# Token-block sums put off, and second-stage loads tied to product numbers, in a one-core encoder layer

## The chip, the cores and the metric

The kernel runs on one core of one Trainium2 chip. The metric is the device time of the whole program in microseconds, from runs on the chip. The profile is one execution taken by the hardware profiler, with its times counted from the first instruction of the span.

## What is computed

One layer of an encoder on x of 512 tokens and 1024 columns, in float32:

```
x = x + 0.5 * ffn1(rms(x));  x = x + mixer(rms(x));  x = x + 0.5 * ffn2(rms(x));  x = rms(x)
ffn(h) = (silu(h @ w_gate) * (h @ w_up)) @ w_down        # 1024 -> 2816 -> 1024
```

The mixer is chunked attention beside a pooling mixer, with one input and one output projection. The change does not touch it. It touches the two down projections, `@ w_down`, and the first norm.

## The kernel before

**Numbers.** A float32 operand is split into a high part that TensorE takes as it is and a low rest: ScalarE casts the high part (`split`, L157), VectorE subtracts it (L158). A product of two operands is three matmuls: high by high, high by low, low by high (`mm3`, L274, L275, L276).

**The down projection.** Its inputs are four token blocks A11, A12, A21, A22 (two halves of the tokens by two halves of the 2816 inner columns) and four weight blocks. The class `Down` forms the result from seven block products with sums of blocks (a scheme of the Strassen kind). Sums of weight blocks, T1 to T4, are made in DRAM by DMAs from POOL's queue (`make_sums`, L939; tile `wsum`). Sums of token blocks, S1 to S4, are made by VectorE. Each block product runs over six groups of the inner dimension (`G` is 6). A group holds two blocks of 128 inner rows, the last holds one, so its products are half as long. Products are counted by `n_products`:

- 1 to 18: for each group g the products S2 by T2, A11 by B11, S1 by T1, into the accumulators `p6`, `p1`, `p5`
- 19 to 30: S3 by T3 (into `p7`) and S4 by B22 (into `p5`), in turn, so 19, 20, 22, 24, 26, 28 are S3
- 31 to 36: A12 by B21 (into `p1`)
- 37 on: A22 by T4 (into `p7`), then the last residual sums, the final norm and the output

**One product.** `product` calls `operands`: `weights` fetches a weight block with a DMA on SP's queue (L965, L968; tile `raw`, up to ten buffers in turn) and splits it into `whi`, `wlo`; `tokens` splits a token block into a pair `ah`, `ah`. Then come the matmuls (`mms`). `tokens` did one thing more: right after the split of S2 and of A11 of a group it issued a sum on VectorE that the later products need, S2 - A12 into S2 (this is S4) or S3 + A11 into S3:

```
if i in (S2, A11):
    dst, other, op = (S2, A12, ALU.subtract) if i == S2 else (S3, A11, ALU.add)
    ...
    nc.vector.tensor_tensor(dst, dst, other, op=op)        # L1002
```

That is two sums for each of six groups, twelve in each stage.

**Buffers.** Token pairs take two buffers of the pool `norm` (tag `h`, 16 buffers of one size). In the second stage the eight rows `xt` of the residual, reloaded from DRAM (`x_d`), take one buffer each of the same pool and keep it. Split weights have four places (`part_tiles`).

**Order.** A tile framework schedules instructions by a model of their times, and inserts the waits. Inside `tc.manual_schedule(engines=...)` the named engines keep the program's order. In products 1 to 18 of both stages, and in the rest of the first stage, SP keeps it; in products 19 on of the second stage SP was scheduled freely. VectorE, ScalarE and TensorE are scheduled freely in the products, but not in the up stage ahead of them. `tc.issue_after(ins)` ties the instructions in its block behind `ins` on the engine of `ins`.

**Reloads.** `self.loads` is a list of DMAs that `product` issues on SP behind the product's weight load (L1028): in the second stage one at each product past 4 whose number leaves 0 or 2 when divided by 3, so 5, 6, 8, 9, 11, 12, 14, 15 for `xt[6]`, `xt[7]`, `xt[2]`, `xt[4]`, `xt[3]`, `xt[5]`, `xt[0]`, `xt[1]`, and 17, 18 for the two rows of the final gain (`gb`). In the first stage it is the input x, one tile each at 15, 18, up to 36. Behind product 19 VectorE scales and adds the accumulators (`scaled`, L1037; `residual`, L1769, into `xt[6]` and `xt[7]`). One piece of `todo` behind each of products 20 to 25 then adds `u2` into `xt[2]`, `xt[4]`, `xt[6]`, `xt[3]`, `xt[5]`, `xt[7]`.

**First norm.** In the opening, `read_in` makes 24 times three matmuls over three pairs of input blocks and lists the last matmul of each three in `made`. The sums of the norm over rows (`per_token`, L389, eight matmuls of one column) are tied behind `made[14]`, the broadcast over rows (`spread`, L414, two matmuls on the scaled identity of L405) behind `made[19]`.

Of the kernel before, what the change touches and what calls it, by code (L numbers as in the profile page):

```python
# [9 lines left out]
F32 = mybir.dt.float32  # L10
# [3 lines left out]
ALU = mybir.AluOpType  # L14
# [3 lines left out]
P = 128  # L18
D = 1024
S = 512  # L20
# [38 lines left out]
STEP, SWITCH, TURN = 0.02, 0.32, 0.11  # L59
ACT_FIX, DVE_FIX, QK_NORM, NORM = 0.09, 0.1, 3.7538, 3.08  # L60
AHEAD_AT = 8
FIRST_NORM = 14, 19
OPENING = (
    "B0 W1 n0 n1 n2 W2 p W3 p B1 p6 W4 W5 B2 p B3 g0 p2 g1 u0 u1 W6 P20 O1 p m0 p W7 P21 g2 m1 p u2 "
    "L0 m2 L1 F0 F1 h0 F2 h1 F3 p2 h2 p L2 h3 p h4 L3 g3 h5 p O0 F4 "
# [11 lines left out]
def layer(  # L77
# [71 lines left out]
            what(*args)  # L149


    last_cast = [None]

    def split(src, hi, lo, scale=None):

        if scale is None:
            last_cast[0] = nc.scalar.copy(hi, src)  # L157
            nc.vector.tensor_tensor(lo, src, hi.bitcast(F32), op=ALU.subtract)  # L158
        else:
            last_cast[0] = nc.scalar.activation(hi, src, AF.Copy, scale=scale)  # L160
            nc.vector.scalar_tensor_tensor(
                lo, src, scale, hi.bitcast(F32), op0=ALU.mult, op1=ALU.subtract
            )

# [717 lines left out]
    class Down:  # L882
# [36 lines left out]

        def begin(self, pool):  # L920
            self.pool, self.acts = pool, []
            self.raws, self.parts, self.pairs = {}, {}, {}
            self.n_products, self.loads, self.loads_from, self.load_turns = 0, [], 4, (0, 2)
            self.open(range(1))
            rooms[:] = [
                z for tag in ("ra", "rb") for z in ((wpool, "raw", RAW, 1024), (pool, tag, RAW, 2 * S))
            ]
            part_rooms[:] = [(wpool, HILO)] * HILO + [(pool, 1)]
# [59 lines left out]
        def tokens(self, i, g, scale=None):  # L988

            if (i, g) in self.pairs:  # L990
                return self.pairs.pop((i, g))
            n = groups[g][1]
            src = self.acts[g][:, S2 if i == S4 else i].rearrange("p k c -> p (k c)")
            pair = [hpool.tile([P, 2, HT], F32R, tag="h", name=name("ah")) for _ in range(2)]
            split(src, *(z[:, :n, :].rearrange("p k c -> p (k c)") for z in pair), scale)
            if i in (S2, A11):

                dst, other, op = (S2, A12, ALU.subtract) if i == S2 else (S3, A11, ALU.add)
                dst, other = (
                    self.acts[g][:, j].rearrange("p k c -> p (k c)") for j in (dst, other)  # L1000
                )
                nc.vector.tensor_tensor(dst, dst, other, op=op)  # L1002
            return pair

        def mms(self, acc, g, a, w, tts=(0, 1), further=False):
# [9 lines left out]

        def operands(self, g, a, i, scale=None):
            w = self.weights(i, g)
            return self.tokens(a, g, scale), w

        def product(self, acc, g, a, i, further=False, scale=None):  # L1020
            a, w = self.operands(g, a, i, scale)
            self.n_products += 1
            if self.n_products == 12:
                tables(AF.Abs_reciprocal_sqrt, a[0][:, 0, 0:1].bitcast(F32))
            turn = self.n_products % 3
            if self.n_products > self.loads_from and turn in self.load_turns and self.loads:
                dst, src = self.loads.pop(0)
                nc.sync.dma_start(dst, src)  # L1028
            if turn == 1 and self.n_products > 1 and self.steps:
                self.make_sums(last_cast[0], 1)  # L1030
            self.mms(acc, g, a, w, further=further)

    def whole(make):
        return [[(make(), 0, S)] for _ in range(2)]
# [37 lines left out]
    with tc.tile_pool(name="act1", bufs=1, reuse_waits="tile") as apool:  # L1072
        down1.begin(apool)
        down1.open(range(1, G - 3))
        ffn_up(n1, wA1, down1, False)
        p1, p5, p6 = whole(bank), whole(bank), whole(abank)

        with tc.manual_schedule(engines={mybir.EngineType.SP}):
            for g in range(G):
                down1.product(p6, g, S2, T2)  # L1080
                down1.product(p1, g, A11, B11)
                down1.product(p5, g, S1, T1)
                if g == 0:

                    x[:] = residual_tiles()
                    half = KD // 2
                    down1.loads = [(x[k], xT[k]) for k in (*range(half, KD), *range(half))]
                    down1.loads_from, down1.load_turns = 14, (0,)
        with tc.manual_schedule(engines={mybir.EngineType.SP}):
            p7 = whole(abank)  # L1090
            u2 = halved(p6)

            y = [down1.acts[i // 2][:, i % 2].rearrange("p k c -> p (k c)") for i in range(2 * NT)]
            down1.product(p7, 0, S3, T3)
            for tt in range(2):
                scaled(u2[tt], p1[tt][0][0], 0.5, u2[tt], ALU.subtract)
                scaled(y[NT + 2 + tt], p5[tt][0][0], 0.5, u2[tt])
            for g in range(G):
                if g + 1 < G:
                    down1.product(p7, g + 1, S3, T3)  # L1100
                down1.product(p5, g, S4, B22, further=True)

            def add(d):

                tp = bank() if d >= KD // 2 else abank()
                for t in range(NT):
                    nc.tensor.transpose(
                        tp[:, t * P : (t + 1) * P],
                        y[d // 4 * NT + t][:, d % 4 * P : (d % 4 + 1) * P], ident,
                    )  # L1110
                nc.vector.tensor_tensor(x[d], x[d], tp, op=ALU.add)
                n2.add(d)

            for tt in range(2):
                todo.append((scaled, y[NT + tt], p5[tt][0][0], -0.5, u2[tt], ALU.subtract))
                todo.append((scaled, y[NT + 2 + tt], p7[tt][0][0], 0.5, y[NT + 2 + tt]))
            for g in range(G):
                down1.product(p1, g, A12, B21, further=True)
                piece()
            todo.extend((add, d) for d in range(KD // 2, KD))  # L1120
            for tt in range(2):
                nc.scalar.activation(two(y[tt]), back(p1[tt][0][0]), AF.Copy, scale=0.5)
            ahead = down1.operands(0, A22, T4, -1.0)
            for g in range(G):
                a, w = ahead
                if g + 1 < G:
                    ahead = down1.operands(g + 1, A22, T4, -1.0)
                down1.mms(p7, g, a, w, further=True)
                piece()
            for tt in range(2):  # L1130
                scaled(y[2 + tt], p7[tt][0][0], -0.5, u2[tt], ALU.subtract)
            for d in range(KD // 2):
                add(d)
        rooms[:] = [(wpool, "raw", RAW, 1024)]
# [595 lines left out]
    with tc.tile_pool(name="act2", bufs=1, reuse_waits="tile") as apool:  # L1730
# [107 lines left out]
        with tc.manual_schedule(engines={mybir.EngineType.SP}):  # L1838
            for g in range(G):
                down2.product(p6, g, S2, T2)  # L1840
                down2.product(p1, g, A11, B11)
                down2.product(p5, g, S1, T1)
                if g == 0:
                    down2.loads = [(xt[i], x_d[i]) for i in (6, 7, 2, 4, 3, 5, 0, 1)] + [
                        (z, final_gain[:, i * S : (i + 1) * S].to_broadcast([P, S]))
                        for i, z in enumerate(gb)
                    ]

        p7 = whole(abank)
        u2 = halved(p6)  # L1850
        down2.product(p7, 0, S3, T3)
        for tt in range(2):
            scaled(u2[tt], p1[tt][0][0], 0.5, u2[tt], ALU.subtract)
            residual(1, 2 + tt, p5[tt][0][0])
            for i in (2 + tt, NT + tt, NT + 2 + tt):
                op = ALU.subtract if i < NT + 2 else ALU.add
                todo.append((nc.vector.tensor_tensor, xt[i], xt[i], u2[tt], op))
        for g in range(G):
            if g + 1 < G:
                down2.product(p7, g + 1, S3, T3)  # L1860
                piece()
            down2.product(p5, g, S4, B22, further=True)
            piece()
        piece(len(todo))
        for tt in range(2):
            todo.append((residual, 1, tt, p5[tt][0][0], 0, S, -0.5))
            todo.extend((residual, 1, 2 + tt, *at) for at in p7[tt])
            todo.append((settle, 1, tt, 1))
            todo.append((settle, 1, 2 + tt, 1))
        for g in range(G):  # L1870
            down2.product(p1, g, A12, B21, further=True)
            piece(2)
        piece(len(todo))
        for tt in range(2):
            residual(0, tt, p1[tt][0][0])
            settle(0, tt, 0)
# [141 lines left out]
```

## Time and profile before

| what | value |
|---|---|
| median of 3 runs | 808.35 us (807.63 to 808.61) |
| the profiled execution | 808.83 us, its span 807.0 us |
| busy: TensorE matmul, weight load, VectorE, ScalarE, POOL | 797.8, 735.5, 710.3, 503.8, 100.1 us |
| granted TensorE clock, mean | 0.999 of full speed |
| first down stage, product 1 to the end of its matmuls | about 219 to 324 us |
| second down stage, product 1 to the end of its matmuls | about 700 to 800 us |

Busy times are sums over instructions, and matmuls overlap in them: a matmul of 512 columns is shown with 0.38 us, though the next one starts 0.22 us later. So a short wait of TensorE shows as a longer step between two starts rather than as idle time. The time outside the span, 808.83 - 807.0, is the program's start and end.

### The profile page before, as it was taken

What the parts mean: (1) busy time and instruction counts of PE and PEld (TensorE: products, weight loads), DVE (VectorE), ACT (ScalarE), POOL (GpSimd) and SP (SyncE); (2) the same over time, 40 slices, a digit from 0 to 9 for tenths busy, and PEclk for the clock granted to TensorE, in tenths of its full rate; (3) what the DMA queues carried; (4) which work ended last, traced back from release to release, by engine and by line L of the source; (5) the groups of instructions that cost most, each with busy time, mean ns of one, the idle gap of its engine ahead of it and who ended that gap; (6) DMA issues with size and microseconds to landing.
All of it is one profiled execution on the core that took longest, in us unless ns stands there. A gap on an engine that the chain in (4) does not pass through costs nothing.

```text
span 807.0 us, 14153 instructions
## 1 busy us (share of the span) xinstructions
PE 797.8 (99%) x5273; PEld 735.5 (91%) x5273; DVE 710.3 (88%) x1163; ACT 503.8 (62%) x873; POOL 100.1 (12%) x148
## 2 busy tenths in 40 slices
PE   9999999999999999999999999999999999999996
PEld 8889999999988888888878888899999999988886
DVE  7999999899897878876979778999989999896997
ACT  8456555666676657558657756565566655766574
POOL 0111111222011100101111000201121111010100
PEclk9999999999999999999999999999999999999999
DMA  8677778988799973332212137858878888799942
GB/s 311 184 210 203 185 214 247 208 201 216 200 270 314 310 241 105 118 118 92 78 54 79 53 132 250 268 160 224 216 213 230 213 199 210 222 305 339 320 144 104
DMA packets 79414, 160.61 MB, mean 199 GB/s; under 512 B 7393, under 2 KB 30705, under 8 KB 78961
## 3 DMA queue, kind: packets, MB, share of 16 engines
q1 hardware_dynamic: 56256, 113.16, 41.7%
q0 software_dynamic: 22656, 46.14, 27.2%
q8 instruction: 41, 0.67, 0.3%
q10 hardware_dynamic: 432, 0.41, 0.1%
q14 instruction: 29, 0.23, 0.1%
HBM read 153.38 MB, written 50.34 MB: 252 GB/s over the span
## 4 chain that ended last, share of the span: by engine, by line
PE 86%; DVE 7%; ACT 4%; issue 2%; DMA 1%; SPq 0%; DVEq 0%; ACTq 0%
PE mm L274 20%; PE mm L275 20%; PE mm L276 20%; PE a L276 7%; PE a L275 7%; PE a L274 7%; DVE wlo L158 1%; PE a L1518 1%; PE a L1506 1%; ACT prob L1423 1%; ACT prob L1429 1%; ACT whi L1235 1%; PE a L1454 1%; DVE prob L1416 1%; DVE wlo L1237 1%
## 5 line engine op out<-in xcount | busy, mean ns | idle before, releaser
L158 DVE TENSOR_TENSOR wlo<-raw,whi 128x1024 fp32r<-128x1024 f32 (+1 forms) x110 | 120.6, 1107 | 17.7 <-ACT whi L157 17.6
L157 ACT CAST whi<-raw 128x1024 fp32r<-128x1024 f32 (+1 forms) x110 | 103.2, 951 | 38.1 <-PE mm L276 14.8
L939 POOL DMA_DIRECT2D wsum<-in_wB_dram x72 | 70.2, 1086 | 447.8 <-DVE t L843 222.1
L275 PE MATMUL mm<-ha,whi 128*128 128x256 f32 x420 | 115.5, 275 | 0.0
L276 PE MATMUL mm<-ha,wlo 128*128 128x256 f32 x420 | 115.5, 275 | 0.0
L274 PE MATMUL mm<-ha,whi 128*128 128x256 f32 x420 | 115.5, 275 | 0.0
L788 ACT ACTIVATE t<-mm 128x256 f32<-128x256 f32 x105 | 40.4, 385 | 113.6 <-PE mm L276 113.1
L600 DVE TENSOR_TENSOR wlo<-wsum,whi 128x1024 fp32r<-128x1024 f32 x70 | 85.5, 1221 | 9.8 <-ACT whi L595 9.8
L274 PEld LDWEIGHTS mm<-ha,whi 128*128 128x128 f32 x420 | 80.6, 192 | 0.1
L275 PEld LDWEIGHTS mm<-ha,whi 128*128 128x128 f32 x420 | 80.6, 192 | 0.1
L276 PEld LDWEIGHTS mm<-ha,wlo 128*128 128x128 f32 x420 | 80.6, 192 | 0.0
L595 ACT CAST whi<-wsum 128x1024 fp32r<-128x1024 f32 x70 | 70.0, 1047 | 3.7 <-DVE wsum L619 2.0
L275 PE MATMUL mm<-wlo,ah 128*128 128x512 f32 x176 | 67.0, 380 | 0.1
L276 PE MATMUL mm<-whi,ah 128*128 128x512 f32 x176 | 66.7, 379 | 0.0
L274 PE MATMUL mm<-whi,ah 128*128 128x512 f32 x176 | 66.5, 379 | 0.0
L274 PE MATMUL mm<-hhi,whi 128*128 128x512 f32 x168 | 64.5, 384 | 0.0
L600 DVE TENSOR_TENSOR wlo<-raw,whi 128x512 fp32r<-128x512 f32 x70 | 64.1, 955 | 0.0
L275 PE MATMUL mm<-hlo,whi 128*128 128x512 f32 x168 | 63.7, 379 | 0.0
L276 PE MATMUL mm<-hhi,wlo 128*128 128x512 f32 x168 | 63.7, 379 | 0.0
L595 ACT CAST whi<-raw 128x512 fp32r<-128x512 f32 x70 | 57.9, 828 | 1.9 <-PE mm L275 1.9
L158 DVE TENSOR_TENSOR ah<-acts,ah 128x512 fp32r<-128x512 f32 (+1 forms) x72 | 45.7, 646 | 10.9 <-ACT ah L157 10.8
L157 ACT CAST ah<-acts 128x512 fp32r<-128x512 f32 (+1 forms) x72 | 40.6, 581 | 20.4 <-PE mm L275 13.8
(246 smaller groups left out, 2331.6 us busy)
## 6 DMA issues: line engine op xcount, KB each, us to landing
raw<-in_wA_dram SPq DMA_DIRECT2D x142, 256.0 KB, 3.9
wsum<-in_wB_dram POOLq DMA_DIRECT2D x60, 512.0 KB, 7.2
raw<-wsum SPq DMA_DIRECT2D x40, 512.0 KB, 6.3
raw<-in_wB_dram SPq DMA_DIRECT2D x30, 512.0 KB, 8.4
wsum<-wsum POOLq DMA_DIRECT2D x20, 512.0 KB, 5.7
raw<-in_wA_dram SPq DMA_DIRECT2D x16, 512.0 KB, 4.6
x<-in_xT_dram SPq DMA_DIRECT2D x16, 256.0 KB, 6.4
raw<-in_wQK_dram SPq DMA_DIRECT2D x8, 512.0 KB, 3.4
```

What stands on the lines that cost most here:

```text
L157: last_cast[0] = nc.scalar.copy(hi, src)
L158: nc.vector.tensor_tensor(lo, src, hi.bitcast(F32), op=ALU.subtract)
L274: nc.tensor.matmul(acc, a[0], b[0], start=start, stop=False, **more)
L275: nc.tensor.matmul(acc, a[0], b[1], start=False, stop=False, **more)
L276: return nc.tensor.matmul(acc, a[1], b[0], start=False, stop=stop, **more)
L595: nc.scalar.copy(hi, src)
L600: nc.vector.tensor_tensor(lo, src, hi.bitcast(F32), op=ALU.subtract)
L788: nc.scalar.activation(two(dst), back(src), AF.Copy, scale=scale)
L939: begun = nc.gpsimd.dma_start(self.rows(i, g), self.rows(self.terms[i][at], g), **(dict(accum_op=ALU.add) if at else {}),)
L1235: nc.scalar.copy(hi, raws[i])
L1237: nc.vector.tensor_tensor(lo, raws[i], hi.bitcast(F32), op=ALU.subtract)
L1416: nc.vector.tensor_tensor_reduce(p, sc, bias[h][0][:, S - n :], -1.0, BIG, op0=ALU.add, op1=ALU.min, accum_out=nm)
```

## The change

It has four parts. The token-block sums are no longer issued in `tokens`; they are put into a list `put_off`, and from the seventh product on each call of `operands` takes one from it and ties it behind the last low-part subtraction (`last_low`). The reloads are given by a table from product number to DMA: in the second stage `RELOADS`, in the first stage 15 + 3 i. Products 19 to 36 of the second stage now stand inside the manual order of SP. The first entry of `FIRST_NORM` goes from 14 to 15.

```diff
-FIRST_NORM = 14, 19
+FIRST_NORM = 15, 19
+RELOADS = 5, 6, 16, 17, 22, 23, 26, 27, 29, 30
...
     def split(src, hi, lo, scale=None):
...
-            nc.vector.tensor_tensor(lo, src, hi.bitcast(F32), op=ALU.subtract)
+            last_low[0] = nc.vector.tensor_tensor(lo, src, hi.bitcast(F32), op=ALU.subtract)
...
-            nc.vector.scalar_tensor_tensor(
+            last_low[0] = nc.vector.scalar_tensor_tensor(
...
         def begin(self, pool):
...
-            self.raws, self.parts, self.pairs = {}, {}, {}
-            self.n_products, self.loads, self.loads_from, self.load_turns = 0, [], 4, (0, 2)
+            self.raws, self.parts, self.pairs, self.put_off = {}, {}, {}, []
+            self.n_products, self.loads = 0, {}
...
         def tokens(self, i, g, scale=None):
...
-                nc.vector.tensor_tensor(dst, dst, other, op=op)
+                self.put_off.append((dst, dst, other, op))
...
         def operands(self, g, a, i, scale=None):
             w = self.weights(i, g)
-            return self.tokens(a, g, scale), w
+            a = self.tokens(a, g, scale)
+            if self.n_products > 5 and self.put_off:
+                *z, op = self.put_off.pop(0)
+                with tc.issue_after(last_low[0].ins):
+                    nc.vector.tensor_tensor(*z, op=op)
+            return a, w
...
         def product(self, acc, g, a, i, further=False, scale=None):
...
-            if self.n_products > self.loads_from and turn in self.load_turns and self.loads:
-                dst, src = self.loads.pop(0)
-                nc.sync.dma_start(dst, src)
+            if self.n_products in self.loads:
+                nc.sync.dma_start(*self.loads[self.n_products])
...
-                    down1.loads = [(x[k], xT[k]) for k in (*range(half, KD), *range(half))]
-                    down1.loads_from, down1.load_turns = 14, (0,)
+                    down1.loads = {
+                        15 + 3 * i: (x[k], xT[k]) for i, k in enumerate((*range(half, KD), *range(half)))
+                    }
...
         with tc.manual_schedule(engines={mybir.EngineType.SP}):
...
                 if g == 0:
-                    down2.loads = [(xt[i], x_d[i]) for i in (6, 7, 2, 4, 3, 5, 0, 1)] + [
-                        (z, final_gain[:, i * S : (i + 1) * S].to_broadcast([P, S]))
-                        for i, z in enumerate(gb)
-                    ]
+                    down2.loads = {
+                        n: (xt[i], x_d[i]) for n, i in zip(RELOADS, (6, 7, 2, 4, 3, 5, 0, 1))
+                    } | {
+                        n: (z, final_gain[:, i * S : (i + 1) * S].to_broadcast([P, S]))
+                        for i, (n, z) in enumerate(zip(RELOADS[8:], gb))
+                    }
...
```

What follows in the second stage, from `p7 = whole(abank)` to the `piece(len(todo))` behind products 31 to 36, is moved inside that `with` block line by line, and is otherwise the same.

## Rows read from the trace of the kernel before

**Rows 1.** The page's busy time by engine, and a costly group (busy, mean ns).

```profile
PE 797.8 (99%) x5273; PEld 735.5 (91%) x5273; DVE 710.3 (88%) x1163; ACT 503.8 (62%) x873; POOL 100.1 (12%) x148
...
L157 ACT CAST whi<-raw 128x1024 fp32r<-128x1024 f32 (+1 forms) x110 | 103.2, 951 | 38.1 <-PE mm L276 14.8
```

**Rows 2.** Timeline of TensorE, second down stage (start us, duration us).

```profile
712.99 0.59 PE L274 MATMUL mm<-whi,ah 128*128 128x512 f32 x2
713.71 0.48 PE L275 MATMUL mm<-wlo,ah 128*128 128x512 f32 x1
714.03 0.38 PE L276 MATMUL mm<-whi,ah 128*128 128x512 f32 x1
...
726.33 0.38 PE L274 MATMUL mm<-whi,ah 128*128 128x512 f32 x1
...
743.16 0.38 PE L274 MATMUL a<-whi,ah 128*128 128x512 f32 x1
...
745.75 0.38 PE L274 MATMUL a<-whi,ah 128*128 128x512 f32 x1
...
746.52 0.48 PE L276 MATMUL a<-whi,ah 128*128 128x512 f32 x1
```

**Rows 3.** Timeline of TensorE, first down stage.

```profile
221.60 0.46 PE L275 MATMUL mm<-wlo,ah 128*128 128x512 f32 x1
221.90 0.38 PE L276 MATMUL mm<-whi,ah 128*128 128x512 f32 x1
```

**Rows 4.** Timeline of TensorE, opening.

```profile
20.10 0.38 PE L276 MATMUL mm<-hhi,wlo 128*128 128x512 f32 x1
20.73 1.05 PE L389 MATMUL a<-ones,acc 128*128 128x1 f32 x8 [0.25 <-DVE acc L385]
...
24.96 0.66 PE L414 MATMUL a<-t,ones_r 128*128 128x512 f32 x2
```

**Rows 5.** Timeline of VectorE, second down stage.

```profile
708.48 0.69 DVE L1002 TENSOR_TENSOR acts<-acts 128x512 f32<-128x512 f32 x1
...
709.68 0.42 DVE L1002 TENSOR_TENSOR acts<-acts 128x256 f32<-128x256 f32 x1
710.02 1.90 DVE L158 TENSOR_TENSOR ah<-acts,ah 128x512 fp32r<-128x512 f32 x3
711.82 0.69 DVE L1002 TENSOR_TENSOR acts<-acts 128x512 f32<-128x512 f32 x1
712.42 1.23 DVE L158 TENSOR_TENSOR wlo<-raw,whi 128x1024 fp32r<-128x1024 f32 x1
...
743.45 1.28 DVE L1769 SCALAR_TENSOR_TENSOR xt<-mm,xt 128x512 f32<-128x512 f32 x2
...
745.77 0.69 DVE L158 TENSOR_TENSOR ah<-acts,ah 128x512 fp32r<-128x512 f32 x1
```

**Rows 6.** Windows: us, busy PE, PEld, DVE, ACT, POOL, clock, DMA share, GB/s.

```profile
730.00:735.00 5.00, 5.00 (x25) 4.38 (x24) 0.85 (x2) 1.43 (x3) 0.52 (x1) 1.00 0.94 333
```

**Rows 7.** Waits of the SP queue, 700 to 745 us (total, times, longest).

```profile
SPq L1028 <- PE mm L276: 14.0, 4, 5.4
```

**Rows 8.** Timeline of the SP queue, second down stage.

```profile
720.34 1.21 SPq L965 DMA_DIRECT2D raw<-wsum  x2
726.31 0.32 SPq L1028 DMA_DIRECT2D xt<-x_d  x1
...
729.52 1.42 SPq L965 DMA_DIRECT2D raw<-wsum  x1
```

**Rows 9.** The instructions of line 1002 (ns min/median/max, first and last start).

```profile
L1002 DVE TENSOR_TENSOR acts<-acts x24: 423/686/696, 93.9 to 732.4; 128x512 f32<-128x512 f32 x20, 128x256 f32<-128x256 f32 x4
```

**Rows 10.** Line 965, weight loads of the second stage: landing.

```profile
DMA to landing us min/median/max: 3.3/7.5/11.8
```

**Rows 11.** DMA issues from 724 to 736 us (count, KB, median us to landing).

```profile
raw<-in_wB_dram SPq DMA_DIRECT2D x2, 512.0 KB, 9.9
```

**Rows 12.** Timeline of VectorE, opening.

```profile
22.86 0.16 DVE L397 TENSOR_SCALAR v<-a 128x4 f32<-128x4 f32 x1
...
24.40 0.68 DVE L405 TENSOR_TENSOR t<-ident,r_lo 128x512 fp32r<-128x512 f32 x1
```

More of the change, by code (lines that the diff above doesn't have):

```diff
@@ L149, in piece @@
             what(*args)
-    last_cast = [None]
+    last_cast, last_low = [None], [None]
     def split(src, hi, lo, scale=None):
@@ L1843, in layer @@
                 if g == 0:
-                    down2.loads = [(xt[i], x_d[i]) for i in (6, 7, 2, 4, 3, 5, 0, 1)] + [
-                        (z, final_gain[:, i * S : (i + 1) * S].to_broadcast([P, S]))
-                        for i, z in enumerate(gb)
-                    ]
[L1849 to L1857, printed above, removed]
@@ L1858, in layer @@
-        for g in range(G):
-            if g + 1 < G:
-                down2.product(p7, g + 1, S3, T3)
-                piece()
[L1862 to L1872, printed above, removed]
@@ L1873, in layer @@
-        piece(len(todo))
+                    down2.loads = {
[4 more added lines that the diff above has]
+                    }
+            p7 = whole(abank)
+            u2 = halved(p6)
+            down2.product(p7, 0, S3, T3)
+            for tt in range(2):
+                scaled(u2[tt], p1[tt][0][0], 0.5, u2[tt], ALU.subtract)
+                residual(1, 2 + tt, p5[tt][0][0])
+                for i in (2 + tt, NT + tt, NT + 2 + tt):
+                    op = ALU.subtract if i < NT + 2 else ALU.add
+                    todo.append((nc.vector.tensor_tensor, xt[i], xt[i], u2[tt], op))
@@ new lines, in layer @@
+            for g in range(G):
+                if g + 1 < G:
+                    down2.product(p7, g + 1, S3, T3)
+                    piece()
+                down2.product(p5, g, S4, B22, further=True)
+                piece()
+            piece(len(todo))
+            for tt in range(2):
+                todo.append((residual, 1, tt, p5[tt][0][0], 0, S, -0.5))
+                todo.extend((residual, 1, 2 + tt, *at) for at in p7[tt])
+                todo.append((settle, 1, tt, 1))
+                todo.append((settle, 1, 2 + tt, 1))
@@ L1874, in layer @@
+            for g in range(G):
+                down2.product(p1, g, A12, B21, further=True)
+                piece(2)
+            piece(len(todo))
         for tt in range(2):
```

## The prediction

> **What bounds the kernel now.** I began with the page: TensorE is busy for 797.8 of 807.0 us [rows 1]. That column hides short waits, because matmuls overlap, so I read TensorE's timeline in both down stages, start by start. A product of twelve 512-column matmuls takes 2.59 us, product 19 from 743.16 to 745.75 [rows 2], so one matmul starts every 0.216 us; an excess over that pace is a wait. From 690 us to the end I find only two above 0.1 us. Before product 6 of the second down stage two matmuls start at 712.99, the next was due at 713.42 and starts at 713.71, and one more 0.32 later: 0.29 + 0.10 = 0.39 us [rows 2]. In product 20 the third matmul was due at 746.19 and starts at 746.52, with the same slow step behind it: 0.33 + 0.10 = 0.43 us [rows 2]. In the first down stage the former place costs 0.08 us [rows 3], the latter nothing. In the opening the first norm's sums start at 20.73 where 20.32 was due: 0.41 us [rows 4]. Everything that the diff can remove adds to 1.3 us. So the question is whether it removes these waits, and whether it makes others.
>
> Who was late? VectorE. Ahead of product 6 it runs without a gap, and three of the sums (L1002), at 708.48, 709.68 and 711.82, stand before the weight split of 712.42 that TensorE waits for [rows 5]. By their start-to-start pace a sum costs 0.60 us, the one of half size 0.34. At product 20 the queue is a split, two L1037, two L1769 from 743.45, a split, and the token remainder of 745.77 [rows 5], which TensorE's third matmul needs. The cause of that one lies earlier: VectorE is busy for only 0.85 us of 730 to 735 [rows 6]. The SP queue shows why: a reload of the residual stands until a token buffer is free, 14.0 us for one cause alone from 700 to 745 [rows 7], and what is behind it stands too. After the eighth reload SP sends ten loads and two gain rows in ten microseconds from 729.52 [rows 8].
>
> **The sums.** There are twelve in each stage, 24 in all, from 93.9 to 732.4 us [rows 9], and none is dropped. Four per stage (S3 + A11 of groups 1 to 4) run today inside the up stage, the first at 93.9, because nothing ties them. After the change all twelve follow the token splits of products 7 to 18, one each. So products 1 to 6 of the second stage are spared the three sums above and one more of full size: 3 x 0.60 + 0.34 = 2.14 us, against 0.39 us of lateness. I count 0.39 us gained. Bounds: 0 if token splits of later products, which nothing ties, are drawn into the free places (three stand there already, at 710.02 [rows 5]), and 0.39 if not. The spared time is five times the wait, so I take the upper end. In products 7 to 18 VectorE then has 1.13 + 0.60 + 0.60 = 2.33 us for a full product against TensorE's 2.59. That covers the sums by 0.26 us each; without the cover one would cost up to 0.60. In the first stage the same takes away its 0.08 us.
>
> **The reloads.** Rows `xt[6]`, `xt[7]` stay at products 5 and 6. The other six move from 8, 9, 11, 12, 14, 15 to 16, 17, 22, 23, 26, 27, the gains from 17, 18 to 29, 30. No DMA is added. There are 16 token buffers; a token pair takes two, a reload keeps one. By the trace they are given in program order: at product 14, with six reloads out, five pairs (10 to 14) fill the rest, and the seventh reload leaves at 726.31 [rows 8] as product 11 begins at 726.33 [rows 2], that is, as product 10's pair comes free. The other five of the six agree. By the same count SP will run freely from product 6 to 16, then stand until TensorE ends product 10 (about 726), and later 11, 17, 18, 22 and 23. The loads of products 9 to 16 leave well before 726, those of 17 to 22 between 726 and 731, in place of the burst from 729.52. So VectorE should not starve at 730, the split ahead of L1037 is done before 740, and L1037 and L1769 begin when products 17 and 18 end. L1769's second half needs the end of product 18, 743.16 - 0.39 = 742.8; with 0.60 + 1.13 + 0.60 us and about 0.1 of hand-over behind each step the remainder for product 20 is ready at about 745.4, due at 746.19 - 0.39 = 745.8. I count 0.33 of the 0.43 us; bounds 0 (both L1769 still stand before the split) and 0.43.
>
> What is queued behind a standing SP? The load of 23 leaves at about 741.9 (product 17 ends a half product of 1.30 before 742.8, then the reload is issued, 0.32), that of 27 at about 753.5 (product 22 ends at 742.8 + 4 x 2.59 = 753.1). TensorE wants them at 753.1 and 763.5. With 2.2 us for cast and split (0.95 [rows 1], 1.13 [rows 5], hand-over) the landing may take 9.0 and 7.8 us. Landings measured 3.3 to 11.8 us, median 7.5 [rows 10]; the long ones belong to the burst, 9.9 there [rows 11]. With SP still from about 744 to 753 few transfers will be out. I cost this at nothing, and keep 11.8 - 7.8 = 4.0 us as the other end. From 753 on ten loads and two gain rows remain, some 5 MB; at 333 GB/s [rows 6] that is 15 us, and product 36 begins only at about 784.
>
> The Trainium skill, page "DMA: Bandwidth & Descriptors", section "Rules for kernel authors", speaks against this part: a DMA is to be issued early, and its semaphore waited on late. By that rule the six reloads lose by moving. The trace disagrees for the place where they stood, since there the early ones held SP [rows 7].
>
> **Program order on SP.** Today the loads of products 19 and 20 are pulled ahead to 720.34 [rows 8]; all later ones already follow the program. Without the pull they leave at about 729, wanted at 743. Nothing.
>
> **The first norm.** `made[15]` puts three matmuls (0.65 us) ahead of the eight small ones, so that the accumulator is no longer waited for: the spread could come 0.41 us earlier than 24.96 [rows 4]. But its second matmul reads the low half of the scaled identity, which VectorE starts at 24.40 and ends at 25.08 [rows 12]; it runs at about 25.18 now. VectorE's row chain begins at 22.86 [rows 12], behind two splits and not behind TensorE. So about 0.06 us is left. Bounds: +0.41 if that chain moves up, a loss of 1.0 if one more split of 1.13 us gets ahead of it.
>
> The first stage's reloads keep their products (15, 18, to 36): nothing.
>
> **Sum.** 0.39 + 0.08 + 0.33 + 0.06 = 0.86 us. The profiled execution took 808.83 us for its span of 807.0, so it would take 807.97; the median of the runs is 808.35, 0.48 below it, which gives 807.5.
>
> **Rivals.**
> *One wait stays.* The two L1769 stand before the split of product 20 with or without DMA, and today VectorE has no gap there [rows 5]. Against it: the first down stage has two operations of that size in the same place, and no wait. Then 808.35 - 0.53 = 807.8.
> *The late loads set the end (slower).* Place: products 23 and 27, behind the reloads of 22 and 26. For it: a median landing of 7.5 us against 7.8 allowed [rows 10]. Against: the long ones come from bursts. Price: the landing less 7.8 us, so 2.1 at the burst's 9.9 and 4.0 at 11.8; time 809.6 to 811.5. It decides from 8.7 us on, where it has eaten the gain. The rule of the Trainium skill quoted above (page "DMA: Bandwidth & Descriptors", section "Rules for kernel authors") would have this outcome.
> *The first norm's chain is cut.* A split goes ahead of it: 1.0 us lost in place of 0.06 gained, 808.6.
> *The edits do nothing.* VectorE's order is the scheduler's, and other splits fill the places that the sums leave, so that both waits stay: 808.35 - 0.14 (the 0.08 and 0.06) = 808.2.
>
> **How the numbers follow.** My forecast 0.50 (its own range 806.9 to 808.0), one wait stays 0.16, late loads 0.13, norm cut 0.08, no effect 0.07, an order that I have not foreseen 0.06. Less than 0.2% (1.62 us) cannot be told from no change here. All waits that I found add to 1.3 us, so a larger gain needs what I do not see, or scatter: faster 0.08. Late loads that land after more than 10.3 us, and the unforeseen, give slower 0.14; same 0.78. The range of 806.6 to 809.4 leaves out most of the late loads and the unforeseen.
>
> **What would show it.** L1002 twelve times in each stage within products 7 to 18, and none in the up stages; no late step of TensorE at products 6 and 20; `xt` reloads on SP near 726, 728, 741.5, 743, 753 and 756; no idle VectorE near 730; the spread still at about 25. I am wrong if TensorE waits in products 21 to 30 for `wlo` while ScalarE waits for `raw`, if VectorE waits for `xt`, or if the opening grows by a microsecond.

## The result and the profile after

The changed kernel takes 810.72 us (median of 10 runs, 809.62 to 811.29), the kernel before 808.31 us beside it (10 runs, 807.63 to 809.23). The ratio is 1.0028 (95% interval 1.0018 to 1.0037): slower by 2.3 us by the ratio. The forecast of 807.5 us with its range up to 809.4 missed. The time lies in the span of the rival "the late loads set the end", 809.6 to 811.5.

The profiled execution of after took 810.58 us for a span of 808.7, against 808.83 and 807.0. Cut at marks in TensorE's timeline (the broadcast of the first norm, the first matmul of each stage, the last matmul), the spans compare like this:

| stretch, us | before | after |
|---|---|---|
| start to the broadcast of the first norm | 24.96 | 24.70 |
| to the first down product | 193.80 | 193.74 |
| first down stage | 102.21 | 102.13 |
| mixer | 170.07 | 170.07 |
| second up stage | 208.88 | 208.88 |
| second down stage, to the last matmul | 100.66 | 102.75 |
| from there to the end | 6.47 | 6.44 |

Only the second down stage lost. Its timeline on TensorE, answering to [rows 2], from product 6 (712.51), 20 (744.89), 23 (752.66) and 31 (772.63):

```profile
712.51 0.59 PE L275 MATMUL mm<-whi,ah 128*128 128x512 f32 x2
712.95 0.38 PE L276 MATMUL mm<-wlo,ah 128*128 128x512 f32 x1
...
744.89 0.38 PE L275 MATMUL a<-whi,ah 128*128 128x512 f32 x1
...
745.32 0.38 PE L277 MATMUL a<-whi,ah 128*128 128x512 f32 x1
...
752.66 0.59 PE L275 MATMUL mm<-whi,ah 128*128 128x512 f32 x2
754.83 0.48 PE L276 MATMUL mm<-wlo,ah 128*128 128x512 f32 x1 [1.57 <-DVE wlo L159]
755.15 0.38 PE L277 MATMUL mm<-whi,ah 128*128 128x512 f32 x1
...
772.63 0.44 PE L275 MATMUL mm<-whi,ah 128*128 128x512 f32 x1
773.84 0.48 PE L276 MATMUL mm<-wlo,ah 128*128 128x512 f32 x1 [0.78 <-DVE wlo L159]
```

The waits at products 6 and 20 are gone: their third matmuls start 0.44 and 0.43 us behind the first, on the pace. Two new ones stand behind `wlo`, the low part of split weights: at product 23 the next start was due 0.43 us after 752.66 and comes 1.74 late, with a slow step of 0.10 behind it, 1.84 us; at product 31 0.99 + 0.10 = 1.09 us. Together 2.93, less the 0.39 and 0.43 that went: 2.11, and the stage is 2.09 longer.

The SP queue, answering to [rows 8], shows the reloads where they were forecast, and what leaves behind them:

```profile
740.98 0.32 SPq L1033 DMA_DIRECT2D xt<-x_d  x1
741.35 0.43 SPq L966 DMA_DIRECT2D raw<-in_wB_dram  x1
742.49 0.32 SPq L1033 DMA_DIRECT2D xt<-x_d  x1
742.90 0.38 SPq L966 DMA_DIRECT2D raw<-wsum  x1
...
752.64 0.32 SPq L1033 DMA_DIRECT2D xt<-x_d  x1
753.01 0.74 SPq L966 DMA_DIRECT2D raw<-in_wB_dram  x1
757.28 0.32 SPq L1033 DMA_DIRECT2D xt<-x_d  x1
```

The loads of 741.35 and 742.90 are those of products 23 and 24. **Product 23.** VectorE and ScalarE ahead of it:

```profile
747.00 1.22 DVE L159 TENSOR_TENSOR wlo<-raw,whi 128x1024 fp32r<-128x1024 f32 x1
748.14 0.68 DVE L159 TENSOR_TENSOR ah<-acts,ah 128x512 fp32r<-128x512 f32 x1
748.74 0.68 DVE L150 TENSOR_TENSOR xt<-xt,t 128x512 f32<-128x512 f32 x1
749.34 0.68 DVE L159 TENSOR_TENSOR ah<-acts,ah 128x512 fp32r<-128x512 f32 x1
749.95 1.28 DVE L150 TENSOR_TENSOR xt<-xt,t 128x512 f32<-128x512 f32 x2
751.15 1.89 DVE L159 TENSOR_TENSOR ah<-acts,ah 128x512 fp32r<-128x512 f32 x3
752.96 0.68 DVE L150 TENSOR_TENSOR xt<-xt,t 128x512 f32<-128x512 f32 x1
753.56 2.35 DVE L159 TENSOR_TENSOR wlo<-raw,whi 128x1024 fp32r<-128x1024 f32 x2
```

```profile
747.46 0.62 ACT L158 CAST ah<-acts 128x512 fp32r<-128x512 f32 x1 [1.97 <-PE a L276]
750.05 0.62 ACT L158 CAST ah<-acts 128x512 fp32r<-128x512 f32 x1 [1.97 <-DVE ah L159]
750.58 2.00 ACT L158 CAST whi<-raw 128x1024 fp32r<-128x1024 f32 x2
```

747.00 is the split of product 22, 753.56 those of 23 and 24 in one row. Between them VectorE does nine other operations without a gap: five token remainders `ah`, those of products 22 to 26, and four pieces of the residual. On ScalarE the cast of 23 stands behind token casts that themselves wait, 1.97 us each, for TensorE and for VectorE. So this does not look like a late transfer. The landing of 23's own load is not in the trace; the load of 24, issued 1.55 us later, landed 5.3 us after its issue, at 748.2, and its cast began after 750.58:

```profile
raw<-wsum SPq DMA_DIRECT2D x1, 512.0 KB, 5.3
```

**Product 31** does look like one. ScalarE waits for the DMA, and VectorE for ScalarE (this row is ScalarE's):

```profile
771.48 1.05 ACT L158 CAST whi<-raw 128x1024 fp32r<-128x1024 f32 x1 [3.40 <-DMA raw<-in_wB_dram]
```

Its load left at 760.18 and landed some 11.2 us later. It is part of a burst: SP had stood until 757.28, and then sent everything. The SP queue's waits of the reloads from 700 to 800 us (to be held against [rows 7]), windows (columns as in [rows 6]), and the issues of 757 to 768 us with their landings:

```profile
SPq L1033 <- PE mm L277: 14.9, 4, 8.9
SPq L1033 <- PE a L277: 14.3, 2, 10.3
SPq L1033 <- DVE ah L159: 8.3, 3, 4.6
```

```profile
740.00:745.00 5.00, 5.00 (x25) 4.38 (x24) 5.00 (x7) 4.93 (x8) 0.42 (x1) 1.00 0.66 208
745.00:750.00 5.00, 5.00 (x25) 4.38 (x24) 5.00 (x8) 1.11 (x2) 1.15 (x2) 1.00 1.04 361
...
755.00:760.00 5.00, 5.00 (x24) 4.38 (x25) 3.78 (x4) 0.71 (x3) 0.00 (x0) 1.00 0.58 195
```

```profile
raw<-in_wB_dram SPq DMA_DIRECT2D x6, 512.0 KB, 11.7
```

The reloads hold SP for 14.9 + 14.3 + 8.3 = 37.5 us. The DMA engines are not idle through all of that: while SP stands from 744.3 to 752.6 they work off what was sent before and what POOL sends (1.04 of 745 to 750 us). They run dry at the end of a stand, 0.02 of 741 to 742 and 0.00 of 757 to 758 us, which lowers the windows to 0.66 and 0.58. Then everything leaves at once, and the loads of half a megabyte take 11.7 us, where one of the same size took 5.3.

**The opening**, answering to [rows 4] (TensorE) and [rows 12] (VectorE):

```profile
21.22 0.95 PE L390 MATMUL a<-ones,acc 128*128 128x1 f32 x8
...
24.70 0.59 PE L415 MATMUL a<-t,ones_r 128*128 128x512 f32 x2
```

```profile
22.50 0.16 DVE L398 TENSOR_SCALAR v<-a 128x4 f32<-128x4 f32 x1 [0.46 <-ACT root L397]
...
24.05 0.68 DVE L406 TENSOR_TENSOR t<-ident,r_lo 128x512 fp32r<-128x512 f32 x1
```

The wait before the norm's sums is gone, and VectorE's row chain starts at 22.50 where it began at 22.86.

### The profile page after: what moved, and what is told of

It reads as the page before. It is cut to its first block, busy times and chain, and to the rows that moved or that the text cites. A ratio compares the mean times of both kernels' runs of the same rounds, so it can differ in the third digit from the quotient of the medians.

```text
span 808.7 us, 14138 instructions
## 1 busy us (share of the span) xinstructions
PE 797.6 (99%) x5273; PEld 735.7 (91%) x5273; DVE 710.8 (88%) x1163; ACT 503.7 (62%) x873; POOL 100.1 (12%) x148
## 5 line engine op out<-in xcount | busy, mean ns | idle before, releaser
L158 ACT CAST ah<-acts 128x512 fp32r<-128x512 f32 (+1 forms) x72 | 40.5, 581 | 22.0 <-PE a L276 10.3
```

## The experiments

Theory A says that the fixed order of VectorE and ScalarE makes the wait at product 23. Theory B says that the late landing behind a reload does. Theory C says that the put-off sums crowd VectorE. Results, with the second down stage from one profile of each (the ratio is an estimate from all runs, not the quotient of the two medians):

| kernel | median, us | before beside it | ratio (95%) | second down stage |
|---|---|---|---|---|
| e1 early reloads | 808.36 | 808.75 | 0.9998 (0.9989 to 1.0007) | 99.94 |
| e2 late reloads alone | 812.92 | 808.75 | 1.0054 (1.0042 to 1.0067) | 102.84 |
| e3 free queue | 809.32 | 808.75 | 1.0004 (0.9995 to 1.0013) | 101.85 |
| e4 pinned | 809.33 | 808.75 | 1.0009 (1.0000 to 1.0018) | 101.55 |
| e5 first pair early | 808.71 | 808.43 | 1.0003 (0.9995 to 1.0012) | 100.70 |
| e6 second pair early | 809.33 | 808.43 | 1.0007 (0.9998 to 1.0016) | 101.60 |
| e7 put off alone | 808.40 | 808.43 | 0.9997 (0.9988 to 1.0006) | 99.94 |
| e8 early, norm 14 | 808.26 | 808.43 | 0.9996 (0.9987 to 1.0005) | 101.30 |
| e9 gains late | 807.65 | 808.26 | 0.9993 (0.9984 to 1.0002) | 99.93 |
| e10 early, again | 808.16 (one run) | 808.26 | | 100.57 |
| e11 changed, again | 810.04 (one run) | 808.26 | | 102.14 |
| e12 split first | 809.40 | 808.55 | 1.0011 (1.0002 to 1.0020) | 101.49 |

The start of the program differs by over a microsecond between these profiles (the matmul ahead of the first norm's sums, or of the three that `made[15]` adds, starts between 19.44 and 20.68; at 20.36 and 19.62 in two of the changed kernel). So a stage is compared by the profiles, and the whole by the ratios.

### Which part lost: e1 and e2

e1 is the changed kernel with the products of before for the reloads:

```diff
-RELOADS = 5, 6, 16, 17, 22, 23, 26, 27, 29, 30
+RELOADS = 5, 6, 8, 9, 11, 12, 14, 15, 17, 18
```

> The changed kernel with the reloads at the old products (5, 6, 8, 9, 11, 12, 14, 15, gains at 17, 18); sums put off, program order and first norm stay changed. Both theories that blame the late reloads, A (their standing in the queue changes the order in which VectorE and ScalarE are scheduled) and B (the loads behind them land late), expect the waits in products 23 (1.8 us) and 31 (1.1 us) to go and the one in product 20 (0.4 us) to come back: 807.4 us, 0.9 under the kernel before. Theory C, that the twelve sums crowded into products 7 to 18 make VectorE late, expects no change: 810.7 us.

The second down stage has no wait above 0.1 us (0.08 + 0.10 are left at product 20, where 0.4 was expected), and is 2.81 us shorter than after, 0.72 shorter than before. The late reloads are the whole loss. C falls: twelve sums in products 7 to 18 cost nothing there.

e2 takes the other half, the late reloads and SP's program order without the other two parts:

```diff
-FIRST_NORM = 15, 19
+FIRST_NORM = 14, 19
...
-                self.put_off.append((dst, dst, other, op))
+                nc.vector.tensor_tensor(dst, dst, other, op=op)
```

> The kernel before with the late reloads and the program order on SP alone: the sums are issued at once behind their token splits, and the first norm's sums are tied as before. A and B expect the waits in products 23 and 31 as in the changed kernel and the one before product 6 (0.4 us) back: about 811.2 us. C expects about 808.3 us.

The wait at 23 is there again, 1.75 + 0.10 us, so it needs no put-off sum. At product 6 it is 0.88 + 0.10, and product 31 has none. So the wait at 31 was not as A and B expected. The end behind the last matmul is 1.74 us longer (8.21): SP's last two stores leave at the same distance from the last matmul as before, 2.58 and 3.00 us, but the later one lands 3.7 us after its issue in place of 1.8. No run shows why. The ratio of e2 holds this end, too, so the late reloads are judged by its stage.

### The order, the queue: e3 and e4

e3 moves products 19 to 36 out of SP's manual order again (the four levels of indentation are all of its edit). e4 adds VectorE and ScalarE to the manual order of those products:

```diff
+        with tc.manual_schedule(engines={mybir.EngineType.SP, mybir.EngineType.DVE, mybir.EngineType.Activation}):
             p7 = whole(abank)
...
```

> The changed kernel with products 19 to 36 outside SP's manual order, as before the change; reloads at the new products. If the program's order on SP is needed for the loss, loads pass the reloads that wait for a token buffer, and both waits go: 807.5 us. If the late place alone makes it, the scheduler leaves the order, and the time stays at 810.7 us.

> The changed kernel with VectorE and ScalarE in program order, too, in products 19 to 36, so that no token split or piece of a later product stands ahead of the weight split of product 23. A (order) expects the 1.8 us in product 23 to go, and the 1.1 us in product 31, which follow a burst on the DMA queue, to stay: 808.9 us. B (late landing) expects both to stay: 810.7 us or more.

Neither expectation of e3 came out. It recovers 0.90 of the 2.09 us: the waits at 23 and 31 are gone, but product 24 has a new one of 1.59 + 0.39 + 0.10. It has a third cause: VectorE stands for the landing of a reload itself, with the split of 24 behind that addition:

```profile
754.74 0.69 DVE L150 TENSOR_TENSOR xt<-xt,t 128x512 f32<-128x512 f32 x1 [4.01 <-DMA xt<-x_d]
755.35 1.22 DVE L159 TENSOR_TENSOR wlo<-raw,whi 128x1024 fp32r<-128x1024 f32 x1
```

e4 has no wait at 23 and 31, but new ones at 19 (0.34) and 20 (1.22 + 0.10), where its rigid order puts four additions ahead of a split. With a slow step of 0.10 at 21 TensorE therefore comes to product 23 some 1.8 us later, so e4 doesn't decide between A and B.

### Two waits, two causes: e5 and e6

```diff
-RELOADS = 5, 6, 16, 17, 22, 23, 26, 27, 29, 30
+RELOADS = 5, 6, 16, 17, 11, 12, 26, 27, 29, 30        # e5
+RELOADS = 5, 6, 16, 17, 22, 23, 14, 15, 29, 30        # e6
```

> The changed kernel with the two reloads of products 22 and 23 moved to 11 and 12; those of 16, 17, 26, 27 and the gains stay late. A (a reload that stands in the SP queue puts later work ahead of product 23 in the orders of VectorE and ScalarE): the wait before product 23 (1.84 us) goes, the one before product 31 (1.09 us), whose load leaves in the burst behind the reloads of 26 and 27, stays; second down stage 102.75 - 1.8 = 100.9 us, time 808.9. B (any late reload makes the next load late): the wait at 23 is replaced by one of like size behind the reloads at 26 and 27, stage 102 to 103 us. If the two waits have one cause, both go: 99.9 us.

> The changed kernel with the two reloads of products 26 and 27 moved to 14 and 15; those of 16, 17, 22, 23 and the gains stay late. A: the wait before product 23 (1.84 us) stays; without the stand of SP from 753 to 757 there is no burst, the load of product 31 lands in time and its 1.09 us go: second down stage 102.75 - 1.1 = 101.7 us, time 809.6. If both waits come from how many reloads stand in all, both change: 100 to 101 us.

Each wait goes with its own pair. In e5 the wait at 23 is gone, and 0.84 + 0.10 us stay at product 31; in e6 1.74 + 0.11 stay at 23, and that at 31 is gone. The stages came to 100.70 and 101.60 where A gave 100.9 and 101.7. VectorE in e5, over the same products (its stage began 0.48 us earlier than in after):

```profile
747.12 1.22 DVE L159 TENSOR_TENSOR wlo<-raw,whi 128x1024 fp32r<-128x1024 f32 x1
748.26 0.69 DVE L159 TENSOR_TENSOR ah<-acts,ah 128x512 fp32r<-128x512 f32 x1
748.86 0.69 DVE L150 TENSOR_TENSOR xt<-xt,t 128x512 f32<-128x512 f32 x1
749.46 1.22 DVE L159 TENSOR_TENSOR wlo<-raw,whi 128x1024 fp32r<-128x1024 f32 x1
```

Between the splits of 22 and 23 stand one remainder and one piece where after has five and four; 23 is split at 749.46.

### The sums alone, and the first norm: e7 and e8

e7 is the kernel before with the sums put off and nothing else (the lines of the diff for `last_low`, `put_off` and `operands`). e8 is e1 with `FIRST_NORM = 14, 19`.

> The kernel before with the token-block sums put off to products 7 to 18 and nothing else: reloads, SP order and first norm as before. The prediction's steps: the waits before product 6 go in both stages (0.39 and 0.08 us), the one in product 20 (0.43 us) stays, since it came from the early reloads and the burst: second down stage 100.66 - 0.39 = 100.27 us, 807.9 in all. Rival: the early-reload kernel of the first runs had no wait in product 20 either, so the sums were its cause: then 99.9 us. Rival C (sums crowd VectorE in products 7 to 18): a new wait there.

> The kernel of early reloads (the changed one with the reload products of before) with the first entry of the first norm back at 14. The second down stage should stay at 99.94 us, the first at 102.13. The norm part was forecast at 0.06 us: the broadcast at 24.9 to 25.0 us against 24.7 with 15, time within 0.3 us of the early-reload kernel's. Rival: the 15 costs time in the opening (its first sum matmuls start later), then this kernel is 0.4 us faster or more, about 807.8.

e7: the first down stage is 102.13 again, product 6 has no wait, and product 20 has 0.18 us left of 0.43, as in e1. By its number, 99.94, that is the rival (the sums as the cause of the wait at 20); e8 speaks against it, where the sums are put off, too. There VectorE, ScalarE and SP hold the very same instructions in the same order as in e1, yet products 19 and 20 wait, and the stage is 1.36 us longer. What differs is the landing of the loads issued from 728 to 742 us, e1 first, then e8:

```profile
raw<-wsum SPq DMA_DIRECT2D x5, 512.0 KB, 9.0
raw<-in_wB_dram SPq DMA_DIRECT2D x4, 512.0 KB, 10.8
```

```profile
raw<-wsum SPq DMA_DIRECT2D x5, 512.0 KB, 10.1
raw<-in_wB_dram SPq DMA_DIRECT2D x4, 512.0 KB, 11.7
```

In e8 ScalarE waits for one of them ahead of product 19, where e1 has no such wait:

```profile
739.60 1.05 ACT L158 CAST whi<-raw 128x1024 fp32r<-128x1024 f32 x1 [1.26 <-DMA raw<-wsum]
```

So the waits at 19 and 20 that go with early reloads are a draw of each execution; e10 below bears that out with the very kernel of e1.

### What repeats: e9, e10, e11

e9 is e1 with the two gain rows alone late (`RELOADS = 5, 6, 8, 9, 11, 12, 14, 15, 29, 30`); e10 and e11 are e1 and the changed kernel once more.

> The kernel of early reloads with the two gain rows alone at products 29 and 30. In two executions of one and the same order of VectorE, ScalarE and SP the burst behind the eighth reload landed in 9.0 and 10.8 us (no wait in products 19 and 20) and in 10.1 and 11.7 us (waits of 1.35 us there); the gain rows are two of the DMAs in that burst. If the landing sets that wait, then without them the loads of products 17 to 19 land earlier, products 19 and 20 have no wait over 0.1 us and the second down stage takes 99.9 us; the gains land unseen. If the wait comes from the order of VectorE there (two L1042 and two L1775 ahead of a split), it stays as likely as before. Time 807.8 either way within 0.5 us.

> A second profile of the early-reload kernel, unchanged. If the wait in products 19 and 20 is set by landings that differ from execution to execution, the second down stage lies anywhere from 99.9 to 101.3 us; waits at products 23 and 31 stay absent, since no reload stands there.

> A second profile of the changed kernel. A (order): the wait before product 23 is 1.84 us again, within 0.05, because the order of VectorE and ScalarE sets it and not a landing. The wait before product 31 hangs on a landing of 11.2 us in the burst and may lie anywhere from 0.5 to 1.5 us. Second down stage 102.2 to 103.2 us. If both come out alike within 0.05 us, landings play no part at product 31 either.

e10 took 100.57 us in the stage, between e1 and e8, with 0.82 us at product 20 alone. e9 has 0.18 us left at 20, as e1 has, its loads landing in 10.3 and 10.4 us; one profile each doesn't show that the gain rows made a difference. In e11 TensorE waits like this:

```profile
752.64 0.59 PE L275 MATMUL mm<-whi,ah 128*128 128x512 f32 x2
754.81 0.48 PE L276 MATMUL mm<-wlo,ah 128*128 128x512 f32 x1 [1.57 <-DVE wlo L159]
...
772.61 0.38 PE L275 MATMUL mm<-whi,ah 128*128 128x512 f32 x1
773.27 0.48 PE L276 MATMUL mm<-wlo,ah 128*128 128x512 f32 x1 [0.28 <-DVE wlo L159]
```

Product 23 repeats to the hundredth, 1.74 + 0.10, as an order would (e2 and e6 have it within 0.01, too); product 31 falls from 1.09 to 0.55 us, as a landing would, and the stage of 102.14 is just under the range. The landing is there: the load of 31 landed at 771.38 in after, 770.82 in e11 and 768.92 in e5 (11.2, 10.4 and 9.6 us after its issue), and the matmul that waits starts 2.46, 2.45 and 2.44 us later. In e2 it landed at 771.77, 2.6 us before that matmul was due, and there is no wait.

### The order by itself: e12

The late reloads stay, the load of 23 leaves SP at 741.57; only VectorE and ScalarE are told to take a product's weights before its tokens.

```diff
-            a = self.tokens(a, g, scale)
+            if self is down2 and 20 < self.n_products < 30:
+                with tc.issue_after(last_cast[0].ins), tc.issue_after(last_low[0].ins):
+                    a = self.tokens(a, g, scale)
+            else:
+                a = self.tokens(a, g, scale)
```

> The changed kernel with its late reloads and its SP order untouched; in products 22 to 30 of the second stage alone the split of a product's tokens is tied behind the split of its own weights on ScalarE and on VectorE. Up to product 22 the order of all engines stays. A (the order set product 23's wait): VectorE's split of 23 moves ahead of the remainders of products 24 to 27, from 753.56 to about 751, in time for the 753.1 at which TensorE wants it; the wait of 1.84 us goes, though the load still leaves SP behind the reload, at about 741.4. B (the load's landing set it): the cast waits for its DMA in the new place and a wait of 1 us or more stays at product 23. The wait before product 31 is a landing in the burst and stays between 0.5 and 1.1 us. Second down stage 100.4 to 101.0 us by A, 101.5 to 102.7 by B; time 808.8 by A, 810 by B.

The wait at 23 is gone. VectorE's split of 23 starts at 750.76 instead of 753.56, and ScalarE's cast already at 745.60, so the load had landed within 4.0 us. That settles A for product 23. Against the forecast the stage is 101.49 us all the same: product 31 lost its wait (its load landed in 6.5 us, at 765.85), but product 29 has a new one. TensorE, then VectorE, before product 29 (L1779 is the residual addition, L1775 of after):

```profile
767.12 0.59 PE L275 MATMUL mm<-whi,ah 128*128 128x512 f32 x2
768.98 0.70 PE L276 MATMUL mm<-wlo,ah 128*128 128x512 f32 x2 [1.27 <-DVE wlo L159]
```

```profile
767.11 0.69 DVE L1779 SCALAR_TENSOR_TENSOR xt<-a,xt 128x512 f32<-128x512 f32 x1 [5.12 <-PE a L277]
767.71 1.21 DVE L159 TENSOR_TENSOR wlo<-raw,whi 128x1024 fp32r<-128x1024 f32 x1
```

VectorE stands for 5.12 us in front of an addition that needs the end of product 28, with the split of 29 behind it, whose cast was done by 763. Again it is the order, at another place.

## Why the prediction was wrong

**The step that failed** is the price of what is queued behind a standing SP: "I cost this at nothing". It measured 1.84 + 1.09 = 2.93 us in the profile, 1.84 + 0.55 in the second one. A premise beside it failed, too: "few transfers will be out" while SP stands, where the DMA engines were busy for 1.04 of 745 to 750 us.

For product 23 the price was asked of the wrong thing. The reckoning by landings held: the load left at 741.35 (forecast 741.9), had 9.0 us by the prediction, and landed within 4.0 in e12; its neighbour took 5.3 in after. What failed is that the order of VectorE and ScalarE was taken as given. That order is made beforehand. With the late reloads it has work for later products ahead of the split of 23, and that work could not be passed over when the load came early enough. e5 and e6 show that the reloads of 22 and 23 make that order, e11 that it costs the same each time, e12 that the order alone is the cost. That the scheduler made it because it reckons with the reload standing in the queue is likely, but not shown: no run shows how it reckons its times.

For product 31 it was a landing, as the rival said, but at another place. The rival looked at the first load behind each reload (23, 27); product 27 had no wait. The loss came four products later, to a load in the burst that follows the stand, 11.2 us to land. The prediction saw the 5 MB that remain from 753 on and set their 15 us against product 36 at 784, the last of them, instead of against each product on the way. The bound of 11.8 us that the rival used for the landing was about right. That the measured time lies in the rival's span is luck for the most part: 1.84 of the 2.93 us belong to "an order that I have not foreseen", which had 0.06, and 1.09 to a place that the rival didn't name. Nor did the signs of being wrong fit: at product 23 ScalarE does not wait for `raw`, and product 31 lies outside the products named.

**The steps that held, or were off in size.** *Sums:* 0.39 at product 6 and 0.08 in the first down stage, measured 0.39 and 0.08, with no price in products 7 to 18 (e7, e1). The spare time behind it was smaller than the 2.14 us reckoned: two sums still stand ahead of the split of product 6, at 709.30 and 710.50, and against the start of the stage that split moves from 712.42 to 711.10, by 0.92 us; it was enough. Four sums less in the second up stage changed nothing, 208.88 both times. *Product 20:* 0.33 of 0.43 forecast, 0.43 gained in the profile. The cause given, the burst behind early reloads, is borne out: with early reloads the stage took 99.94, 99.94 and 99.93 us (e1, e7, e9), 100.57 (e10) and 101.30 (e8), all of the difference in products 19 and 20, and of the profiles with late ones only the pinned e4 waits there. So the 0.43 was one draw; the six profiles with early reloads have 0.18 to 1.55 us there. *First norm:* 0.06 forecast. From the matmul ahead of the place of `made[14]` to the first down product it took 198.66 us before and 198.08 after, 0.58 gained, of which 0.41 is the wait and the rest smaller ones; but over four profiles with 14 the mean is 198.48, over ten with 15 198.29. So about 0.2 us is the likelier size, which so few profiles don't fix: 198.08 is the shortest of both, in six of the ten and in one of the four. The premise that failed is that the row chain begins "behind two splits and not behind TensorE": in after VectorE is through with the splits and waits 0.46 us for ScalarE's `root`, which itself waits for TensorE's sums, so the chain moved up, the case of the upper bound of 0.41. *Reload times:* five of six within 0.6 us; the last, behind the wait at 23, left at 757.28 instead of 756.

**The sum again:** 0.39 + 0.08 + 0.43 + 0.58 - 2.93 = -1.45 us; the opening began 0.26 us later in this execution; -1.71 against the spans' -1.7. The chance of 0.13 for the late loads was too small above all because only a landing was taken to bring them about. The row of the standing SP, which spoke for moving the reloads, misled: with the late reloads the stand didn't shrink but grew, to 37.5 us over the stage from 14.9 + 8.3 = 23.2 in e1. The Trainium skill's rule, page "DMA: Bandwidth & Descriptors", section "Rules for kernel authors", is to issue a DMA early and wait late. The sign of e1 agrees with it, by 2.81 us in the stage, though the larger part of that came by an order and not by a transfer that was too late.

**A version to keep** is e9, with the sums put off and the rows `xt` reloaded early: 807.65 us, faster than the changed kernel, and not told apart from before (0.9984 to 1.0002).

## What to carry to other kernels

Moving a DMA in a queue that keeps program order can change the order that a scheduler fixes for other engines: look at what it put ahead of the operation that needs the transfer, not only at whether the transfer lands in time. Behind a stand comes a burst, and each load in it has to be set against its own product, with the burst's landing time. Short waits that hang on landings differ between executions of one program, so take a second profile before a wait under a microsecond is put into a sum.

## What the runs showed that was not expected

Two executions with the same order of instructions on VectorE, ScalarE and SP (e1, e8) differed by 1.36 us in one stage, through landings of 9.0 and 10.8 against 10.1 and 11.7 us. And pushing the wait of 1.84 us at product 23 away without moving the reloads moved it: some 1.8 us at 19 to 21 (e4), 2.1 at 24 (e3), or 1.7 at 29 (e12); only moving the reloads gave it back.
